# Transfers within DRAM at other places, single-bank PSUM tiles, and an earlier split of operand sums, in a hybrid encoder step

## The chip, the cores and the metric

The kernel runs on one core of one Trainium2 chip. The metric is the device time of one execution in microseconds. The core has a matrix engine (TensorE, PE in the profile), a vector engine (VectorE, DVE), an engine for activations (ScalarE, ACT), a general engine (GpSimd, POOL) and a sequencer that issues transfers (SyncE, SP). Transfers from GpSimd go by a queue that software fills (q0 in the profile), those from SyncE by a hardware queue (q1).

## The reference

One step of a one-layer streaming encoder on 512 prompt frames and 32 frames of a running stream. Half of the mixer's heads are a gated recurrence, half are latent attention; then comes a convolutional FFN.

```python
def token_mixer(x, s0, lat_past, kr_past, ...):
    hq, hf, hi, hg, cq, ckv, kr = jnp.split(x @ w_in, SPLITS, axis=-1)
    f = lb + (1.0 - lb) * jax.nn.sigmoid(hf)
    o_h, s_new = hgrn2_recurrence(heads(hq), heads(1.0 - f), heads(jnp.log(f)), heads(hi), s0, blk)
    o_h = rms_norm(o_h, hgrn_norm_g) * jax.nn.silu(hg)
    ...
    o_a = mla_attention(q_nope, q_rope, k_nope, krs, v, q_pos, k_pos)
    out = jnp.concatenate([o_h, o_a], axis=-1) @ w_out
    return out, s_new, lat_new, kr_new

h = layer_norm(x)
h = layer_norm(ALPHA * h + token_mixer(h))
h = layer_norm(ALPHA * h + conv_ffn(h))
```

`w_in` is 2048 x 4928, `w_out` 2048 x 2048, and the FFN is 5632 wide; everything is float32.

## The kernel before

**Precision and tiling.** The 544 frames lie along the free dimension, as two halves of 272. Each float32 operand is split into a high and a low part (`aH`, `aL` for activations, `wh`, `wl` for weights: a copy to `fp32r` on ScalarE, a subtraction on VectorE), and each product is three matmuls, high by high, high by low and low by high (`mm3`, L146).

**Stages** (by the timeline of the profiled execution): input norm and the query latent until about 80 us; the key and value latent and the rotary key (`ckv_proj`, `kr_proj`, `head_qf(0)`) until 141; four pairs of attention heads, `proj_pair` woven with `attend`, and `head_ig(0)` until about 305; the levels of the first recurrence heads with the sums of inputs (`load_sums` L721 and L722, `sums_of_inputs` with the subtractions of L181) until 371; the recurrence with the divided input projection until about 710; the first column group of the output projection (`out_first`) until 745; the rest of the output projection until about 866; then the FFN (L1313, L1344). In the recurrence, each head's norm takes a power on GpSimd (L995).

**Divided products.** Some projections are computed block by block with sums of weight blocks and sums of activations, so that a 2 x 2 block product takes seven products in place of eight. In the input projection the summed weights are formed in SBUF by accumulating DMAs of GpSimd (L782 in `form`, L795 in `low`). For the output projection, sixteen summed blocks of `w_out` (`wf_dr`) are formed inside DRAM by 32 transfers, a copy or an accumulate of 512 KB each (`forming`, L79 to L97). They come in six phases: eight copies, eight accumulates, then four each of copies, accumulates, copies and accumulates. `form_next` issues the next one. All of them go out on GpSimd: 16 from `tick` in the attention stage, every fourth step (L672 to L687), and 16 from `low` behind the accumulate of product s2: two each time while more than eight are left, then one.

**The block products of the output projection.** Eight steps of `five` and `six` (`step`, L1467 on) compute column groups five and six plainly for the first half of the frames, beside the first norm sums (`Norm.first`, L1121 to L1149). Then `play` runs the list `oitems`, one `Product` (L1794) after the other. Four products "11" come first, one for each group g, and each writes a PSUM tile `X[g]`; `out_sink` (L1825, L1822) adds the result to the residual on VectorE. `ohooks` names what VectorE and ScalarE do after an item: the splits of the summed activations (`split_su`, L1417 and L1418) among them.

**What sets the order.** Inside `manual_schedule` each engine runs what the program writes, in that order. A queue of transfers is in order at its issuing engine. A matmul waits until the earlier readers of its PSUM tile are done, by tile and not by half: X[1] and X[2] are the two halves of one tile of two banks, and X[3] and X[4] of another.

Of the kernel before, what the change touches and what calls it, by code (L numbers as in the profile page):

```python
# [59 lines left out]
def tile_encoder_step(ctx, tc, xp, xs, w_in, w_in4, w_kr, w_q_b, w_kv_b, w_out, w_out4, w_up, w_gate, w_down, w_down2,  # L60
# [24 lines left out]
    def forming(phase):  # L85
        for g in range(1, 5):
            f = {n: wf_dr[g, n] for n in ("s1", "s2", "s3", "22")}
            for out, src, add in ((("s1", "11", False), ("s3", "12", False)), (("s1", "12", True), ("s3", "22", True)),
                                  (("s2", "s1", False),), (("s2", "22", True),), (("22", "s2", False),), (("22", "21", True),))[phase]:
                src = f[src] if src in f and not add else out_block(g, src)  # L90
                yield lambda out=f[out], src=src, add=add: G.dma_start(out, src, **({"accum_op": ALU.add, "max_dma_last_dim": 2048} if add else {}))
# [3 lines left out]
    def form_next(n=0):  # L95
        if len(forms) > n:
            tc.keep_in_program_order(forms.pop(0)())  # L97
# [302 lines left out]
    with tc.tile_pool(name="mp", bufs=1) as mp, tc.tile_pool(name="psa", bufs=4, space=PSUM) as psa:  # L400
# [271 lines left out]
        weave([ckv_proj(), kr_proj()], [cq_norm()], 0.5)  # L672
        weave([head_qf(0)], [ckv_norm(), kr_rope()], 0.5)
        ticks = [0]

        def tick():
            ticks[0] += 1
            if ticks[0] % 4 == 0:
                form_next(16)

        weave([proj_pair(0)], [], 0.0, tick)
        weave([proj_pair(1)], [attend(0)], 2.0, tick)
        weave([proj_pair(2)], [attend(1)], 2.0, tick)
        weave([proj_pair(3)], [attend(2)], 2.0, tick)
        weave([head_ig(0)], [attend(3)], 2.0, tick)
        while len(forms) > 16:
            form_next()  # L687

# [14 lines left out]
    with tc.tile_pool(name="gp", bufs=1) as gp, tc.tile_pool(name="psg", bufs=1, space=PSUM) as psg:  # L703
# [60 lines left out]
        class Divided:  # L764
# [26 lines left out]
            def low(self, wh):  # L791
                wl = wp.tile([P, 1024], R, name="wl", tag="wl")
                V.tensor_tensor(out=wl, in0=self.t(self.key), in1=wh.bitcast(F32), op=ALU.subtract)  # L793
                if self.name == "s2":
                    G.dma_start(self.t("11"), self.src("21"), accum_op=ALU.add)  # L795
                    for _ in range(2 if len(forms) > 8 else 1):
                        form_next()
# [294 lines left out]
    psA = ctx.enter_context(tc.tile_pool(name="psA", bufs=2, space=PSUM))  # L1092
# [383 lines left out]
    early = [psA.tile([P, 1024], F32, name="acc", tag="acc") for _ in range(2)]  # L1476
    with tc.manual_schedule():
# [21 lines left out]
        for j in range(2):  # L1499
# [3 lines left out]
            firsts.append(nrm[j].first(zt[0], zt[1], early[0][:, 512 * j:512 * j + 512]))  # L1503
# [6 lines left out]
        five, six = pair_half(early[1], 0), pair_half(main_tile(), 0)  # L1510
# [286 lines left out]
    with tc.manual_schedule():  # L1797
# [37 lines left out]
        xa, xb = main_tile(), main_tile()  # L1835
        X = {g: (xa, xb)[(g - 1) // 2][:, 512 * ((g - 1) % 2):512 * ((g - 1) % 2) + NI] for g in range(1, 5)}
        BC = [psA.tile([P, 1024], F32, name="acc", tag="acc")[:, 512 * i:512 * i + NI] for i in range(2)]
# [19 lines left out]
        def restore():  # L1857
            for k in range(HK):
# [3 lines left out]
        ohooks = {0: [lambda: split_su("s1", 0), lambda: split_su("s1", 1)], 1: [lambda: split_su("s2", 0)], 2: [lambda: split_su("s2", 1)],  # L1862
                  3: [lambda: split_su("s4", 0)], 4: [lambda: split_su("s4", 1)], 5: [lambda: split_21(range(4))],
                  6: [lambda: split_21(range(4, 8))],
# [8 lines left out]
        oitems[1].prep()  # L1873
# [762 lines left out]
```

## Time and profile before

| | us |
|---|---|
| median of 3 runs | 2353.41 |
| lowest and highest | 2353.05, 2353.92 |
| profiled execution | 2357.51 |
| its span in the profile | 2355.7 |

The page of the profile gives the share of the span in which each engine works, the granted clock of the matrix engine, and the share of time that the 16 DMA engines move something. VectorE works for 73% of the span, ScalarE for 47%, GpSimd for 12%; the DMA engines moved 474.55 MB at a mean of 201 GB/s. In a row of a timeline, the number in square brackets is how long the engine stood idle before, and behind the arrow is what released it. "L1794" is a line of the kernel before.

### The profile page before, as it was taken

What the parts mean: (1) busy time and instruction counts of PE and PEld (TensorE: products, weight loads), DVE (VectorE), ACT (ScalarE), POOL (GpSimd) and SP (SyncE); (2) the same over time, 40 slices, a digit from 0 to 9 for tenths busy, and PEclk for the clock granted to TensorE, in tenths of its full rate; (3) what the DMA queues carried; (4) which work ended last, traced back from release to release, by engine and by line L of the source; (5) the groups of instructions that cost most, each with busy time, mean ns of one, the idle gap of its engine ahead of it and who ended that gap; (6) DMA issues with size and microseconds to landing.
All of it is one profiled execution on the core that took longest, in us unless ns stands there. A gap on an engine that the chain in (4) does not pass through costs nothing.

```text
span 2355.7 us, 44621 instructions
## 1 busy us (share of the span) xinstructions
PE 2304.0 (98%) x18244; PEld 2285.7 (97%) x18244; DVE 1714.7 (73%) x2395; ACT 1095.9 (47%) x1686; POOL 273.9 (12%) x343
## 2 busy tenths in 40 slices
PE   7999999999999999999999999999999999999997
PEld 7999899999999999999999999999999999999996
DVE  7455558777776778987777777777777677777776
ACT  6344434433344536665455554555545433333323
POOL 1011101110111121000010000100001111111102
PEclk9999999999999999999999999999999999999998
DMA  7344475665666655777767667676677999889832
GB/s 245 99 137 128 113 211 166 165 173 165 154 177 229 240 164 201 195 228 192 222 166 227 186 184 222 167 225 187 184 222 185 366 325 306 268 274 301 286 94 78
DMA packets 175772, 474.55 MB, mean 201 GB/s; under 512 B 16080, under 2 KB 80336, under 8 KB 168144
## 3 DMA queue, kind: packets, MB, share of 16 engines
q1 hardware_dynamic: 140112, 316.57, 38.7%
q0 software_dynamic: 35456, 155.14, 28.5%
q8 instruction: 143, 2.34, 0.4%
q14 instruction: 61, 0.50, 0.1%
HBM read 394.36 MB, written 91.34 MB: 206 GB/s over the span
## 4 chain that ended last, share of the span: by engine, by line
PE 90%; DVE 3%; DMA 3%; ACT 2%; issue 1%; POOL 0%; SPq 0%; ACTq 0%; DVEq 0%; POOLq 0%
PE main L1313 21%; PE acc L1313 16%; PE main L1344 10%; PE main L146 10%; PE main L851 10%; PE acc L1344 7%; PE acc L146 3%; PE main L1794 2%; PE s L916 2%; PE acc L1794 2%; PE main L591 1%; PE at L652 1%; DMA cx<-catd 1%; PE at L621 1%; DMA x<-in_xp 1%
## 5 line engine op out<-in xcount | busy, mean ns | idle before, releaser
L1255 DVE TENSOR_TENSOR wl<-raw,wh 128x1024 fp32r<-128x1024 f32 x371 | 456.6, 1231 | 194.4 <-ACT wh L1254 194.1
L1254 ACT ACTIVATE wh<-raw 128x1024 fp32r<-128x1024 f32 x371 | 392.0, 1059 | 410.9 <-PE main L1313 98.4
L1313 PE MATMUL main<-op,wh 128*128 128x272 f32 x1408 | 265.4, 288 | 0.0
L1313 PE MATMUL acc<-ops,wh 128*128 128x272 f32 x1344 | 254.1, 288 | 0.0
L1313 PE MATMUL main<-ops,wh 128*128 128x272 f32 x1344 | 254.1, 288 | 0.0
L1313 PEld LDWEIGHTS main<-op,wh 128*128 128x128 f32 x1408 | 221.1, 188 | 0.0
L1313 PEld LDWEIGHTS acc<-ops,wh 128*128 128x128 f32 x1344 | 211.2, 188 | 0.0
L1313 PEld LDWEIGHTS main<-ops,wh 128*128 128x128 f32 x1344 | 211.1, 188 | 0.0
L1313 PE MATMUL main<-op,wl 128*128 128x272 f32 x704 | 203.1, 289 | 0.3 <-DVE wl L1255 0.3
L1313 PE MATMUL acc<-ops,wl 128*128 128x272 f32 x672 | 194.0, 289 | 0.6 <-DVE wl L1255 0.6
L1313 PE MATMUL main<-ops,wl 128*128 128x272 f32 x672 | 193.9, 289 | 0.0
L1313 PE MATMUL acc<-op,wh 128*128 128x272 f32 x832 | 157.5, 288 | 1.0 <-DVE eg L1619 1.0
L1254 ACT ACTIVATE wh<-rawl 128x1024 fp32r<-128x1024 f32 x93 | 98.8, 1063 | 117.5 <-PE acc L1313 46.1
L146 PE MATMUL main<-aH,wl 128*128 128x272 f32 (+2 forms) x608 | 148.5, 295 | 2.6 <-DVE wl L317 1.8
L146 PE MATMUL main<-aH,wh 128*128 128x272 f32 (+2 forms) x608 | 149.7, 297 | 0.3 <-ACT wh L316 0.2
L146 PE MATMUL main<-aL,wh 128*128 128x272 f32 (+2 forms) x608 | 146.8, 293 | 1.0 <-DVE aL L305 1.0
L1255 DVE TENSOR_TENSOR wl<-rawl,wh 128x1024 fp32r<-128x1024 f32 x93 | 113.8, 1224 | 26.5 <-ACT wh L1254 26.4
L1313 PEld LDWEIGHTS main<-op,wl 128*128 128x128 f32 x704 | 132.4, 188 | 0.5 <-DVE wl L1255 0.5
L1313 PEld LDWEIGHTS acc<-op,wh 128*128 128x128 f32 x832 | 130.6, 188 | 1.2 <-ACT eg L1646 1.2
L793 DVE TENSOR_TENSOR wl<-raw,wh 128x1024 fp32r<-128x1024 f32 x84 | 103.1, 1227 | 35.9 <-ACT wh L788 35.0
L1313 PEld LDWEIGHTS acc<-ops,wl 128*128 128x128 f32 x672 | 126.4, 188 | 0.8 <-DVE wl L1255 0.8
L1313 PEld LDWEIGHTS main<-ops,wl 128*128 128x128 f32 x672 | 126.4, 188 | 0.0
(495 smaller groups left out, 6108.7 us busy)
## 6 DMA issues: line engine op xcount, KB each, us to landing
raw<-in_w_in SPq DMA_DIRECT2D x76, 512.0 KB, 5.1
raw<-in_w_up SPq DMA_DIRECT2D x71, 512.0 KB, 5.3
raw<-in_w_gate SPq DMA_DIRECT2D x71, 512.0 KB, 4.8
raw<-in_w_down SPq DMA_DIRECT2D x67, 512.0 KB, 9.4
opd<-ohl SPq DMA_DIRECT2D x20, 1088.0 KB, 5.5
ops<-opd POOLq DMA_DIRECT2D x20, 1088.0 KB, 12.1
raw<-in_w_up POOLq DMA_DIRECT2D x35, 512.0 KB, 5.3
opd<-ohl SPq DMA_DIRECT2D x20, 816.0 KB, 6.5
```

The source lines that it names most:

```text
L146: PE.matmul(ps, ww[:, wcols[0]:wcols[1]], aa[:, hs[j]], start=first and i == 0, stop=last and i == 2, skip_group_check=True)
L591: PE.matmul(ps[:, j * 512:j * 512 + 256], l[k][:, a:b], r4(w[:, k:k + 1, :])[:, 0, :, 128:256], start=k == 0 and i == 0, stop=k == 1 and i ...
L621: PE.matmul(sc[:, :nk], qn[j][:, q0:q0 + P], kn[j][:, :nk], start=True, stop=False)
L652: PE.matmul(po[:, :P], vt[:, k, j, :], t[:, k * P:(k + 1) * P], start=k == 0, stop=k == b)
L793: V.tensor_tensor(out=wl, in0=self.t(self.key), in1=wh.bitcast(F32), op=ALU.subtract)
L851: PE.matmul(out, ww[:, k * P:(k + 1) * P], aa, start=name in ("11", "s1", "12") and k == 0 and q == 0, stop=k == HK - 1 and q == 2, skip_g ...
L916: PE.matmul(ps[:, j * 64:(j + 1) * 64], Kp[:, a:b], Qv[:, j * bt:(j + 1) * bt, 1, :], start=True, stop=True)
L1254: A.activation(wh, src, AF.Copy)
L1255: V.tensor_tensor(out=wl, in0=src, in1=wh.bitcast(F32), op=ALU.subtract)
L1313: PE.matmul(ps, ww[:, k * P:(k + 1) * P], aa, start=self.first and k == 0 and i == 0, stop=k == n - 1 and i == 2, skip_group_check=True)
L1344: PE.matmul(banks[:, 512 * u:512 * u + NI], ww[:, (u * n + k) * P:(u * n + k + 1) * P], aa, start=self.first and k == 0 and i == 0, stop=k ...
L1794: PE.matmul(self.bank, ww[:, k * P:(k + 1) * P], aa, start=self.first and k == 0 and i == 0, stop=k == HK - 1 and i == 2, skip_group_check ...
```

## The change

Three things are altered. The eight copies of the first phase go out on SyncE's queue instead of GpSimd's, at every fifth step of the latent stage; the attention stage issues none of the 32 transfers; and the other 24 go out in pairs at the twelve s2 points of the recurrence. In the block products, the norm's first sums, `five` and the four tiles `X` get four PSUM tiles of a single bank each (`sb0` to `sb3`, pool `psB`), the two-bank pool `psA` is opened after that stage, and `BC` is now two tiles of the main pool. And the two splits of s1 stand ahead of the last additions of `six`, before `play`, while the later hooks each come one item earlier.

```diff
--- before.py
+++ after.py
@@ -88,7 +88,7 @@
             for out, src, add in ((("s1", "11", False), ("s3", "12", False)), (("s1", "12", True), ("s3", "22", True)),
                                   (("s2", "s1", False),), (("s2", "22", True),), (("22", "s2", False),), (("22", "21", True),))[phase]:
                 src = f[src] if src in f and not add else out_block(g, src)
-                yield lambda out=f[out], src=src, add=add: G.dma_start(out, src, **({"accum_op": ALU.add, "max_dma_last_dim": 2048} if add else {}))
+                yield lambda out=f[out], src=src, add=add: (G.dma_start(out, src, accum_op=ALU.add, max_dma_last_dim=2048) if add else (dma if phase == 0 else G.dma_start)(out, src))
 
     forms = [f for phase in range(6) for f in forming(phase)]
 
@@ -669,22 +669,22 @@
             G.tensor_tensor(out=o[:, :, :NI], in0=o[:, :, :NI], in1=o[:, :, NI:], op=ALU.subtract)
             dma(d3_dr[pr], o[:, :, :NI])
 
-        weave([ckv_proj(), kr_proj()], [cq_norm()], 0.5)
-        weave([head_qf(0)], [ckv_norm(), kr_rope()], 0.5)
         ticks = [0]
 
         def tick():
             ticks[0] += 1
-            if ticks[0] % 4 == 0:
-                form_next(16)
-
-        weave([proj_pair(0)], [], 0.0, tick)
-        weave([proj_pair(1)], [attend(0)], 2.0, tick)
-        weave([proj_pair(2)], [attend(1)], 2.0, tick)
-        weave([proj_pair(3)], [attend(2)], 2.0, tick)
-        weave([head_ig(0)], [attend(3)], 2.0, tick)
-        while len(forms) > 16:
+            if ticks[0] % 5 == 0 and len(forms) > 24:
+                form_next()
+
+        weave([ckv_proj(), kr_proj()], [cq_norm()], 0.5, tick)
+        weave([head_qf(0)], [ckv_norm(), kr_rope()], 0.5, tick)
+        while len(forms) > 24:
             form_next()
+        run(proj_pair(0))
+        weave([proj_pair(1)], [attend(0)], 2.0)
+        weave([proj_pair(2)], [attend(1)], 2.0)
+        weave([proj_pair(3)], [attend(2)], 2.0)
+        weave([head_ig(0)], [attend(3)], 2.0)
 
     def out_piece(kk, g):
         return piece(w_out[kk, max(g - 4, 0)], 4, 256)
@@ -793,7 +793,7 @@
                 V.tensor_tensor(out=wl, in0=self.t(self.key), in1=wh.bitcast(F32), op=ALU.subtract)
                 if self.name == "s2":
                     G.dma_start(self.t("11"), self.src("21"), accum_op=ALU.add)
-                    for _ in range(2 if len(forms) > 8 else 1):
+                    for _ in range(2):
                         form_next()
                 elif self.name not in ("11", "s1"):
                     slots.append(self.raw.pop(self.key)[0])
@@ -1089,7 +1089,6 @@
     ph1.close()
 
 
-    psA = ctx.enter_context(tc.tile_pool(name="psA", bufs=2, space=PSUM))
     seq = [0]
 
     def acc_tile():
@@ -1473,7 +1472,11 @@
                     kk == 0 and k == 0, kk == 3 and k == 3)
 
     ko = [CAT_ORDER[4 * kk] // 4 for kk in range(4)]
-    early = [psA.tile([P, 1024], F32, name="acc", tag="acc") for _ in range(2)]
+    psb_stack, psb = stack(tc.tile_pool(name="psB", bufs=1, space=PSUM))
+
+    def small_tile(n):
+        return psb.tile([P, 512], F32, name=f"sb{n}", tag=f"sb{n}")
+
     with tc.manual_schedule():
         order56 = [(kk, g) for g in (5, 6) for kk in ko]
         raws56, ws56 = [], []
@@ -1500,14 +1503,14 @@
             for t in range(2):
                 z = zt[t][:, H_[j]]
                 V.scalar_tensor_tensor(out=z, in0=z, scalar=ALPHA, in1=wo_tiles[t][:, PS_[j]], op0=ALU.mult, op1=ALU.add)
-            firsts.append(nrm[j].first(zt[0], zt[1], early[0][:, 512 * j:512 * j + 512]))
+            firsts.append(nrm[j].first(zt[0], zt[1], small_tile(j)))
             next(firsts[j])
 
         def next_firsts():
             for f in firsts:
                 next(f, None)
 
-        five, six = pair_half(early[1], 0), pair_half(main_tile(), 0)
+        five, six = [small_tile(2 + t)[:, :NI] for t in range(2)], pair_half(main_tile(), 0)
         step(five, ws56[0], 0, 0)
         split_next()
         next_firsts()
@@ -1832,9 +1835,8 @@
             return Product(out_weights(g, name), name, None, bank, name in ("11", "s1", "12"),
                            lambda: out_sink(g, name, bank))
 
-        xa, xb = main_tile(), main_tile()
-        X = {g: (xa, xb)[(g - 1) // 2][:, 512 * ((g - 1) % 2):512 * ((g - 1) % 2) + NI] for g in range(1, 5)}
-        BC = [psA.tile([P, 1024], F32, name="acc", tag="acc")[:, 512 * i:512 * i + NI] for i in range(2)]
+        X = {g: small_tile(g - 1)[:, :NI] for g in range(1, 5)}
+        BC = [main_tile()[:, :NI] for _ in range(2)]
         oitems = [out_item(g, "11", X[g]) for g in range(1, 5)]
         for g in range(1, 5):
             oitems += [out_item(g, name, {"12": BC[0], "s1": BC[1], "s4": BC[1]}.get(name, X[g]))
@@ -1859,9 +1861,8 @@
                 load_21(k, cat_dr[4 + k // 2][:, k % 2, NI:])
 
         NO = len(oitems)
-        ohooks = {0: [lambda: split_su("s1", 0), lambda: split_su("s1", 1)], 1: [lambda: split_su("s2", 0)], 2: [lambda: split_su("s2", 1)],
-                  3: [lambda: split_su("s4", 0)], 4: [lambda: split_su("s4", 1)], 5: [lambda: split_21(range(4))],
-                  6: [lambda: split_21(range(4, 8))],
+        ohooks = {0: [lambda: split_su("s2", 0)], 1: [lambda: split_su("s2", 1)], 2: [lambda: split_su("s4", 0)],
+                  3: [lambda: split_su("s4", 1)], 4: [lambda: split_21(range(4))], 5: [lambda: split_21(range(4, 8))],
                   NO - 2: [lambda: split_seventh(0)],
                   NO - 1: [lambda: split_seventh(1), lambda: [shifted(14 + t, 0) for t in range(2)]]}
         pump()
@@ -1871,6 +1872,8 @@
         oitems[0].prep()
         step(six, ws56[7], 0, 3)
         oitems[1].prep()
+        for i in range(2):
+            split_su("s1", i)
         for t in range(2):
             V.tensor_tensor(out=zt[12 + t][:, H_[0]], in0=zt[12 + t][:, H_[0]], in1=six[t], op=ALU.add)
             fill(0.8, lambda t=t: nrm[0].add(zt[12 + t], G))
@@ -1883,6 +1886,8 @@
             drain(3.0)
 
     ou_stack.close()
+    psb_stack.close()
+    psA = ctx.enter_context(tc.tile_pool(name="psA", bufs=2, space=PSUM))
     st_stack, st = stack(pool("st", "right"))
 
     with tc.manual_schedule():
```

On GpSimd, from the third attention pair to the setup of the recurrence, before (L91 is a transfer within DRAM into a summed block `wf`; L669 is the subtraction at the end of a pair; L560, L462 and L567 belong to the rotary embedding):

```order
L560 COPY ql_964<-t 128x32
L91 DMA wf1s_101<-in_w_out 256x512
L91 DMA wf2s_103<-in_w_out 256x512
L669 TENSOR_TENSOR o<-o 128x2x272
L91 DMA wf2s_105<-in_w_out 256x512
L91 DMA wf3s_107<-in_w_out 256x512
L91 DMA wf3s_109<-in_w_out 256x512
L669 TENSOR_TENSOR o<-o 128x2x272
L91 DMA wf4s_111<-in_w_out 256x512
L91 DMA wf4s_113<-in_w_out 256x512
L708 MEMSET attnT_3489 128x544
L708 MEMSET attnT_3490 128x544
```

The same place of the changed kernel:

```order
L560 COPY ql_964<-t 128x32
L462 TENSOR_TENSOR t<-t,cos 128x544
L567 COPY ql_964<-t 64x32 x2
L560 COPY ql_964<-t 128x32
L669 TENSOR_TENSOR o<-o 128x2x272 x2
L708 MEMSET attnT_3481 128x544
L708 MEMSET attnT_3482 128x544
L711 MEMSET kT 128x128
```

All transfers L91 of this place are gone; they were accumulates, and they stand in the recurrence now.

On GpSimd, the last points s2 of the recurrence, before (L782 and L795 are the accumulates into weights in SBUF, L995 the power in a head's norm, and the last row loads the residual for the output projection):

```order
L782 DMA raw<-in_w_in 128x1024
L795 DMA raw<-in_w_in 128x1024
L91 DMA wf_110<-in_w_out 256x512
L995 TENSOR_TENSOR r_7624<-r_7623,nhalf 128x5
L782 DMA raw<-in_w_in 128x1024
L795 DMA raw<-in_w_in 128x1024
L91 DMA wf_114<-in_w_out 256x512
L995 TENSOR_TENSOR r_8226<-r_8225,nhalf 128x5
L1495 DMA za<-h0d_69 128x544
```

and in the changed kernel:

```order
L91 DMA wf_102<-in_w_out 256x512
L91 DMA wf_106<-in_w_out 256x512
L995 TENSOR_TENSOR r_7623<-r_7622,nhalf 128x5
L782 DMA raw<-in_w_in 128x1024
L795 DMA raw<-in_w_in 128x1024
L91 DMA wf_110<-in_w_out 256x512
L91 DMA wf_114<-in_w_out 256x512
L995 TENSOR_TENSOR r_8226<-r_8225,nhalf 128x5
L1498 DMA za<-h0d_69 128x544
```

Each point has two accumulates within DRAM where it had one, and the last summed block is the second of its pair. The number of points with an L995 behind them stays.

On the matrix engine, the heads of the first two block products, with the semaphores that they wait for (Activation is ScalarE, DVE is VectorE; the first row of each group opens a product), before:

```order
L1794 MATMUL main<-aH,wh 128x272 [waits Activation_49]
L1794 MATMUL main<-aL,wh 128x272
L1794 MATMUL main<-aH,wl 128x272 [waits DVE_49]
...
L1794 MATMUL main<-aH,wh 128x272 [waits DVE_49,Activation_49]
L1794 MATMUL main<-aL,wh 128x272
L1794 MATMUL main<-aH,wl 128x272
```

and in the changed kernel, where L1797 is the former L1794:

```order
L1797 MATMUL sb_8711<-aH,wh 128x272 [waits Activation_49]
L1797 MATMUL sb_8711<-aL,wh 128x272
L1797 MATMUL sb_8711<-aH,wl 128x272 [waits DVE_49]
...
L1797 MATMUL sb_8712<-aH,wh 128x272 [waits Activation_49]
L1797 MATMUL sb_8712<-aL,wh 128x272
L1797 MATMUL sb_8712<-aH,wl 128x272 [waits DVE_49]
```

The second product no longer waits for VectorE at its first matmul; it waits for it two matmuls later, for its low weights, as the first one does.

## The prediction

> **What bounds the kernel now.** I read the page first, then the waits of TensorE (PE), then the granted clock by window, then the timeline around each long wait.
>
> ```profile
> span 2355.7 us, 44621 instructions
> PE 2304.0 (98%) x18244; PEld 2285.7 (97%) x18244; DVE 1714.7 (73%) x2395; ACT 1095.9 (47%) x1686; POOL 273.9 (12%) x343
> ```
>
> PE is busy for 98% of the span, so only two things can shorten the time without removing matmuls: an idle gap of PE, or a stretch in which its clock is lowered. The waits of PE, as total, count and longest in us, hold five rows that the change can reach:
>
> ```profile
> PE main L1794 <- DVE za L1825: 4.4, 2, 3.8
> PE at L638 <- DVE o L653: 2.4, 1, 2.4
> PE s L916 <- DVE Kp L922: 3.0, 1, 3.0
> PE acc L1126 <- ACT n_cb L1140: 0.5, 1, 0.5
> PE acc L1121 <- DVE nt_c L1136: 0.3, 1, 0.3
> ```
>
> Windows say what follows them. The columns are the length, busy times and counts of the engines, the granted clock (PEclk), the share of the DMA engines, and GB/s:
>
> ```profile
> 240.00:250.00 10.00, 8.35 (x42) 7.45 (x43) 7.80 (x19) 5.68 (x13) 3.02 (x5) 0.83 0.63 131
> ...
> 310.00:320.00 10.00, 7.00 (x50) 6.78 (x49) 6.21 (x16) 2.15 (x5) 2.09 (x4) 0.90 1.03 300
> 320.00:330.00 10.00, 10.00 (x54) 10.00 (x53) 5.31 (x14) 1.49 (x2) 0.00 (x0) 0.59 0.92 275
> 770.00:780.00 10.00, 6.17 (x48) 5.98 (x47) 7.12 (x9) 7.82 (x9) 2.42 (x2) 0.94 1.03 411
> 780.00:790.00 10.00, 9.38 (x54) 9.19 (x54) 5.96 (x7) 3.59 (x4) 0.00 (x0) 0.72 0.73 284
> ```
>
> After each of the three waits of 2.4 us or more the clock falls below 1.00 for a while. A stretch at clock c loses (1 − c) of its length: 0.17 × 10 = 1.7 us behind the wait in attention, 0.10 × 10 + 0.41 × 10 = 5.1 us behind the one at the levels, 0.06 × 10 + 0.28 × 10 = 3.4 us behind the one in the block products, 3.4 on average. So a removed wait is worth itself plus this. By the Trainium skill, page "TensorE: Matmul & The Clock Gate", section "What's actually happening", half rate follows an idle window of about 3.4 us and full rate returns after a busy window of about 3.4 us; the trace differs, since 2.41 us already sufficed here and the clock stayed low longer at the levels. By the page a spell would cost an estimated 1.7 us instead of these measured losses, and the forecast gain would be 10.0 instead of 13.4.
>
> **Block products: single-bank tiles and earlier splits (gain 7.4 + 0.8).**
>
> ```profile
> 772.58 0.28 PE L1794 MATMUL main<-aH,wh 128*128 128x272 f32 x1
> ...
> 775.14 3.06 DVE L1418 TENSOR_TENSOR us<-us 128x1088 fp32r<-128x1088 f32 x2
> ...
> 779.02 0.43 DVE L1825 SCALAR_TENSOR_TENSOR za<-za,main 128x272 f32<-128x272 f32 x1
> 779.36 1.22 DVE L1255 TENSOR_TENSOR wl<-raw,wh 128x1024 fp32r<-128x1024 f32 x1
> ...
> 779.59 0.56 PE L1794 MATMUL main<-aH,wh 128*128 128x272 f32 x1 [3.83 <-DVE za L1825]
> ...
> 780.50 1.28 DVE L1418 TENSOR_TENSOR us<-us 128x1088 fp32r<-128x1088 f32 x1
> ```
>
> The first block product starts at 772.58. The second writes the other half of the same two-bank tile, so it waits until DVE has read the first half (L1825, 779.02), and DVE is held up by two operand splits of s1 (3.06 us for the pair). PE stands for 3.83 us. The fourth product does the same with the second tile:
>
> ```profile
> 789.19 0.36 PE L1794 MATMUL main<-aH,wh 128*128 128x272 f32 x1 [0.62 <-DVE za L1825]
> ...
> 738.62 6.12 PE main L146 x48
> ```
>
> The undisturbed price of a product of 24 matmuls is half of the row of 48 on the chain of waits: 3.06 us. The three products from 772.58 to 789.19 should take 9.18 and took 16.61, so 7.4 us are lost, in idle time and slow clock together. In the new order the waits on VectorE at the heads of products two and four are gone; both write tiles of their own. What is late next? DVE has per product one sink (0.43), one weight split (1.22) and one operand split (1.28), 2.93 us against 3.06 on PE, so it just keeps up, and the weight splits needed for the second product are behind fewer operations than before, since the s1 splits now stand ahead of play. These two splits there run beside the last two steps of `six`, 48 matmuls or 6.1 us, against 2 × 1.5 us. If that cover were gone they would cost 3.06. I take the whole 7.4; the bounds are 0, if DVE stays the bound, and 7.4. The two waits of the norm's first sums (0.5 and 0.3, rows above) come from one shared tile too and go: 0.8, between 0 and 0.8.
>
> **Attention without transfers within DRAM (gain 4.1).**
>
> ```profile
> 227.93 0.94 POOL L91 DMA_DIRECT2D wf1s<-in_w_out  x1
> ...
> 232.89 0.59 SPq L458 DMA_DIRECT2D t<-t  x1
> ...
> 238.67 0.72 DVE L463 TENSOR_TENSOR t<-t,sin 128x544 f32<-128x544 f32 x1 [3.59 <-DMA t<-t]
> ...
> t<-t SPq DMA_DIRECT2D x20, 68.0 KB, 2.1
> ```
>
> The swap of rows for the rotary embedding is issued at 232.89 and DVE gets it at 238.67, 5.8 us later; the median of its kind, from issue to landing, is 2.1 (the last line, from the list of DMA issues). In front of it, at 227.93, GpSimd issued an accumulate within DRAM. DVE stands 3.59 us for the swap, and the attention copy of L653 queued behind it makes PE stand 2.4 (its row among the waits above). At the median the swap would land 3.7 us earlier, more than the stall. Removed: 2.4 + 1.7 of slow clock = 4.1. The bounds are 0 (the swap is late because of the weight loads beside it) and 4.1; I take 4.1, since the accumulate is the only transfer of that kind in that stretch.
>
> **Sums of inputs (gain 7.5).**
>
> ```profile
> 303.06 0.87 POOL L91 DMA_DIRECT2D wf4s<-in_w_out  x1
> ...
> 306.92 1.53 SPq L721 DMA_DIRECT2D s<-h0d  x3
> ...
> 313.10 0.44 DVE L181 TENSOR_TENSOR s_f<-s,s 128x272 f32<-128x272 f32 x1 [4.76 <-DMA s<-h0d]
> ...
> s<-h0d SPq DMA_DIRECT2D x32, 136.0 KB, 3.8
> ```
>
> The same again: an accumulate at 303.06, three loads from 306.92 on, of which the first sum needs two, and DVE standing 4.76 us until 313.10. Behind L181 and its followers on DVE waits L922, and on it PE, 3.0 us (its row among the waits above). The second load is issued at about 307.4; at the median of its kind, 3.8 us (last line), it lands at 311.2, 1.9 us earlier, and at the 2.1 us of the smaller swap at 309.5, 3.6 us earlier. The gain is 1.9 to 3.0 of idle time and 5.1 of slow clock: 7.0 to 8.1, and 0 if the loads delay each other. I take the middle, 7.5.
>
> **What the moved transfers cost where they go.** The eight copies of the first phase are issued on SyncE's queue in the latent stage:
>
> ```profile
> 80.00:141.00 61.00, 60.80 (x490) 60.61 (x489) 27.53 (x45) 17.42 (x25) 5.21 (x4) 1.00 0.36 108
> ```
>
> PE is busy for 60.80 of these 61 us, at full clock and a DMA share of 0.36 (columns as in the windows above). Queued behind the copies on SP are the next weight loads; they are hidden by the weights that are already split, so the cost is 0. Without that cover one copy would delay a load as the swap above was delayed: 3.7 us, with a slow clock 7. In the recurrence, each s2 point now issues two transfers where the last eight points had one. An accumulating pair holds GpSimd:
>
> ```profile
> 439.75 1.26 POOL L91 DMA_DIRECT2D wf1s<-in_w_out  x1
> ...
> 449.41 0.90 POOL L91 DMA_DIRECT2D wf2s<-in_w_out  x1 [8.39 <-issue]
> ...
> 456.39 1.19 POOL L995 TENSOR_TENSOR r<-r,nhalf 128x5 f32<-128x5 f32 x1 [6.08 <-DVE r L994]
> ```
>
> From 439.75 to 450.3 GpSimd is held, 10.6 us, and the next operation that matters there, the power in the head's norm at 456.39 (L995), comes 16.6 us after the first issue. It stays 6 us clear: cost 0; the other end is the last rival's 30. The price is at the last point, where the second accumulate now falls ten microseconds after 687.53, into a stretch that is already full:
>
> ```profile
> 687.53 1.29 POOL L91 DMA_DIRECT2D wf<-in_w_out  x1
> ...
> 690.00:698.00 8.00, 8.00 (x69) 8.00 (x69) 5.94 (x13) 2.48 (x4) 0.00 (x0) 1.00 1.01 200
> 698.00:710.00 12.00, 12.00 (x101) 12.00 (x100) 9.44 (x23) 4.25 (x8) 0.00 (x0) 1.00 1.05 400
> ...
> 708.59 1.07 ACT L134 ACTIVATE wh<-raw 128x1024 fp32r<-128x1024 f32 x1 [3.45 <-DMA raw<-in_w_out]
> ...
> 716.18 0.52 PE L146 MATMUL main<-aH,wl 128*128 128x272 f32 x2 [0.88 <-DVE wl L135]
> ...
> q0 software_dynamic: 35456, 155.14, 28.5%
> ```
>
> The rows are from the timeline, from two windows (columns as above), and from the page's list of queues (packets, MB, share of the span). DMA share is 1.01 at 200 GB/s while the accumulate runs and 1.05 at 400 GB/s after it. ScalarE stands 3.45 us for a weight load at 708.59, and PE has a gap of 0.88 us behind a weight split at 716.18. One more accumulate of 512 KB takes at least 0.524 MB divided by the software queue's own rate, 155.14 MB in 28.5% of 2355.7 us = 231 GB/s: 2.3 us. At most it halves the rate for 8 us, as the first window shows: 4.0 us, and a third more for the read of the target, 5.3. I take 3.0, nearer to the queue's rate, because that rate already contains many accumulates. The gap becomes 3.9 us, and gaps of 2.4 and more were followed by a slow clock, so 3.4 more: −6.4 (bounds 0, hidden, and −10). By the Trainium skill, page "DMA: Bandwidth & Descriptors", section "Issuing engines are not separate DMA queues", transfers run on the same sixteen engines whichever engine issues them. That speaks against this change, which moves load and removes none; the trace agrees as far as the two rates above show. By it alone the sum would be the 1.8 of the second rival below.
>
> **The sum.** 7.4 + 0.8 + 4.1 + 7.5 − 6.4 = 13.4 us. The profiled execution took 2357.5, of which its span is 2355.7, so 2344.1 for it; the median of the runs is 2353.4, 4.1 lower, and the same gain gives 2340.0.
>
> **Rivals.**
> - The extra accumulate at the end of the recurrence is hidden: the last term is 0, and the time 2333.6. For it: PE itself has a gap of only 0.88 us there. Against it: the share of 1.05. 22%.
> - Attention and sums do not improve, because the loads that are late there wait behind 512 KB weight loads and one another on engines that all transfers share, and the accumulates were only a part of it; at the end of the recurrence the cost stays. The gain is 8.2 − 6.4 = 1.8, and the time 2351.6. For it: the share is 1.03 in 310 to 320, at 300 GB/s. Against it: both late transfers follow an accumulate by 4 to 5 us. (This is where the rule of the DMA page leads.) 10%.
> - DVE stays the bound of the block products (2.93 against 3.06 is little room), 7.4 is not had: 2347.4. 12%.
> - Slower: the pairs of accumulates hold GpSimd for 20 us instead of 10.6, and L995 comes late. It decides from a hold of 16.6 us, and at the first call from 13.4:
>
> ```profile
> 384.60 0.84 POOL L91 DMA_DIRECT2D wf1s<-wf1s  x1
> ...
> 397.95 1.18 POOL L995 TENSOR_TENSOR r<-r,nhalf 128x5 f32<-128x5 f32 x1 [12.01 <-DVE r L994]
> ```
>
> Four of the accumulating calls have an L995 behind them. At 20 us the first loses 6.6 and three lose 3.4 each, with a slow clock of 3.4 behind all four: 16.8 + 13.6 = 30.4, and the time is 2370.4. The measured 10.6 speaks against it. 6%.
>
> **How the numbers follow.** The forecast has 50%. The range 2332 to 2351 takes in the forecast with both ends of its terms, the hidden accumulate and the DVE-bound block products, together 84%. A measurement tells 0.2%, or 4.7 us, from no change: faster is below 2348.7, slower above 2358.1. Forecast, first and most of the third rival are faster: 0.80. The second and the rest of the third are the same: 0.13. Slower is the fourth and one hundredth for what I overlooked: 0.07.
>
> **What would show it.** Right would be: no wait of PE on L1825's successor between the first block products and clock 1.00 in 770 to 790; no wait of L638 on L653 and of L916 on L922; and a wait at the first pieces of the output projection longer than 0.9 us. Wrong would be a wait of PE for DVE at another place in the block products, a swap or sum that lands late without an accumulate in front, or L995 with PE waiting behind it.

## The result, and the profile after

The changed kernel takes 2339.99 us (median of 4, 2339.09 to 2340.97) against 2353.66 of the kernel before on the same chip (median of 4, 2353.05 to 2357.07): a ratio of 0.9939, with a 95% interval from 0.9922 to 0.9956. That is 13.7 us. The profiled execution took 2339.57, its span is 2337.8.

The page, and the rows of the waits of the matrix engine that answer to those shown before (total, count, longest, in us):

```profile
span 2337.8 us, 44618 instructions
...
PE 2295.4 (98%) x18244; PEld 2279.1 (97%) x18244; DVE 1713.6 (73%) x2395; ACT 1095.4 (47%) x1686; POOL 271.1 (12%) x335
```

```profile
PE main L1797 <- DVE za L1828: 1.4, 1, 1.4
PE sw L952 <- DVE Kp L922: 1.1, 1, 1.1
...
PE main L146 <- ACT wh L134: 1.0, 1, 1.0
PE main L146 <- DVE wl L135: 0.9, 1, 0.9
```

The rows of L638 on L653 (2.4), of L916 on L922 (3.0) and of the two first sums of the norm (0.5 and 0.3) are gone. The row of the block products has shrunk from 4.4 to 1.4 and is another wait than before: a product that comes five places later. Two rows at the first pieces of the output projection are new or longer: 1.0 on ScalarE, and 1.1 instead of 0.5 on L922.

The windows of before, again with length, busy times, clock, DMA share and GB/s, and one more at the end of the recurrence:

```profile
240.00:250.00 10.00, 10.00 (x67) 8.62 (x66) 6.99 (x22) 6.03 (x14) 0.21 (x1) 1.00 0.41 127
310.00:320.00 10.00, 10.00 (x85) 10.00 (x85) 7.85 (x20) 1.92 (x3) 0.00 (x0) 1.00 0.86 257
320.00:330.00 10.00, 10.00 (x83) 9.79 (x84) 7.95 (x19) 4.46 (x9) 0.00 (x0) 1.00 0.76 239
...
700.00:710.00 10.00, 7.05 (x41) 6.45 (x40) 9.07 (x16) 8.81 (x17) 0.00 (x0) 0.83 0.49 146
770.00:780.00 10.00, 10.00 (x80) 9.80 (x79) 7.74 (x11) 6.64 (x11) 0.00 (x0) 1.00 0.90 346
780.00:790.00 10.00, 8.65 (x70) 8.66 (x70) 8.31 (x15) 5.01 (x8) 0.00 (x0) 1.00 0.60 203
```

The clock is 1.00 in the five windows that had 0.59 to 0.94. It is 0.83 in a new place, 700 to 710. The two transfers that had been late are on time now, by the timeline:

```profile
231.56 0.59 SPq L458 DMA_DIRECT2D t<-t  x1
...
234.40 0.73 DVE L463 TENSOR_TENSOR t<-t,sin 128x544 f32<-128x544 f32 x1 [0.26 <-DMA t<-t]
```

```profile
301.08 1.38 SPq L721 DMA_DIRECT2D s<-h0d  x3
...
304.77 0.44 DVE L181 TENSOR_TENSOR s_f<-s,s 128x272 f32<-128x272 f32 x1 [1.36 <-DMA s<-h0d]
```

The swap is used 2.8 us after its issue (5.8 before), and the first sum starts 3.7 us after the loads are issued (6.2 before).

**Where the time went.** The matrix engine runs the same number of matmuls in both kernels, 18244, so the n-th matmul of one profile can be set beside the n-th of the other. The table gives the difference of their start times (after minus before) at the ends of the stages. A second profile of each kernel (runs e4 and e11 below) gives the second pair. (The output projection's first four products are named "11"; s1 and s4 are later products of a group, and the s4 product is the seventh in order.)

| up to matmul | stage that ends there | first pair | second pair |
|---|---|---|---|
| 110 | start | +0.3 | −0.5 |
| 1700 | attention | −5.2 | −3.6 |
| 2270 | sums and first levels | −13.1 | −9.3 |
| 5680 | recurrence, `out_first` | −10.1 | −5.7 |
| 5730 | first sums of the norm | −10.8 | −6.4 |
| 5950 | first block products | −18.4 | −12.6 |
| 6030 | s4 product of the first group | −16.8 | −11.3 |
| 18000 | FFN | −18.2 | −10.8 |

### The profile page after: what moved, and what is told of

It reads as the page before. It is cut to its first block, busy times and chain, and to the rows that moved or that the text cites. A ratio compares the mean times of both kernels' runs of the same rounds, so it can differ in the third digit from the quotient of the medians.

```text
span 2337.8 us, 44618 instructions
## 1 busy us (share of the span) xinstructions
PE 2295.4 (98%) x18244; PEld 2279.1 (97%) x18244; DVE 1713.6 (73%) x2395; ACT 1095.4 (47%) x1686; POOL 271.1 (12%) x335
## 4 chain that ended last, share of the span: by engine, by line
PE 92%; DVE 2%; ACT 2%; DMA 2%; issue 1%; SPq 0%; POOL 0%; ACTq 0%; DVEq 0%; POOLq 0%
PE main L1312 22%; PE acc L1312 17%; PE main L146 11%; PE main L1343 11%; PE main L851 10%; PE acc L1343 7%; PE acc L146 3%; PE s L916 2%; PE main L1797 1%; PE sb L1797 1%; PE main L591 1%; PE at L652 1%; PE at L621 1%; DMA cx<-catd 1%; DMA xr<-wf1s 1%
```

## The experiments

Ratios are against the kernel before on the same chip, five rounds each; in brackets the 95% interval.

**The three parts alone.** First the transfers:

```diff
-                form_next(16)
...
+            if ticks[0] % 5 == 0 and len(forms) > 24:
+                form_next()
...
-                    for _ in range(2 if len(forms) > 8 else 1):
+                    for _ in range(2):
```

with the copies of the first phase on SyncE, as in the change.

> The transfers within DRAM at their new places, PSUM tiles and split order as before. My theory: the accumulates beside attention are what makes the rotary swap (L458) and the loads of the sums (L721) late. From the matmuls of the two profiles, aligned one by one, attention gives 5.5 us, the sums 7.9, and the end of the recurrence takes back 3.1: a span 10.3 us shorter than the profiled 2355.7, no wait of L638 on L653 and none of L916 on L922, and the wait of the second block product (3.8 us) still there. Rival: the loads delay one another whatever the accumulates do; then the waits on L653 and L922 stay and the gain is under 3 us.

Measured: 2347.08 against 2354.30, 0.9970 (0.9960 to 0.9981), and a span of 2344.9, 10.8 below the profiled 2355.7. By the medians that is 7.2 us. The waits on L653 and L922 are gone, and so is 1.2 us of a wait on a softmax step (L604); the wait of the second block product is still 3.8. The rival falls.

Then the tiles:

```diff
-        five, six = pair_half(early[1], 0), pair_half(main_tile(), 0)
+        five, six = [small_tile(2 + t)[:, :NI] for t in range(2)], pair_half(main_tile(), 0)
...
-        X = {g: (xa, xb)[(g - 1) // 2][:, 512 * ((g - 1) % 2):512 * ((g - 1) % 2) + NI] for g in range(1, 5)}
-        BC = [psA.tile([P, 1024], F32, name="acc", tag="acc")[:, 512 * i:512 * i + NI] for i in range(2)]
+        X = {g: small_tile(g - 1)[:, :NI] for g in range(1, 5)}
+        BC = [main_tile()[:, :NI] for _ in range(2)]
```

> The single-bank PSUM tiles alone; transfers and split order as before. My theory: the shared two-bank tile is the whole cause of the stall, since the low weights of the first three block products are ready before the s1 splits: no wait of PE on L1825 at the second and fourth product, clock 1.00 in 770 to 790, and 7 to 8.4 us shorter (0.8 of it from the norm's first sums). Rival: VectorE is the bound, because two splits of 1.5 us each still stand ahead of the first sink and the weight split behind it; then PE waits for low weights instead of the sink and the gain is under 4 us.

Measured: 2347.28 against 2354.30, 0.9969 (0.9956 to 0.9981). By the medians that is 7.0 us. Both waits of PE at the second and fourth product are gone, and the clock stays up. The only row of a block product that is left, of 0.5, belongs to the s4 product. From its waits, its timeline and its windows:

```profile
PE main L1797 <- DVE za L1828: 0.5, 1, 0.5
```

```profile
789.13 0.49 PE L1797 MATMUL main<-us,wh 128*128 128x272 f32 x2 [0.46 <-DVE za L1828]
```

```profile
770.00:780.00 10.00, 10.00 (x82) 10.00 (x81) 9.15 (x12) 7.61 (x9) 2.41 (x2) 1.00 1.02 408
```

So the shared tile alone was the cause, and VectorE was not the bound of the first four products. The two s1 splits still stand ahead of the first sink here, and cost nothing.

Then the order of the splits:

```diff
+        for i in range(2):
+            split_su("s1", i)
...
-        ohooks = {0: [lambda: split_su("s1", 0), lambda: split_su("s1", 1)], 1: [lambda: split_su("s2", 0)], 2: [lambda: split_su("s2", 1)],
...
+        ohooks = {0: [lambda: split_su("s2", 0)], 1: [lambda: split_su("s2", 1)], 2: [lambda: split_su("s4", 0)],
```

> The earlier s1 splits alone; transfers and tiles as before. My theory: the tile dependence stays, but VectorE reaches the first sink 3.1 us earlier, so that the wait of 3.8 us falls to about 0.8 and, being that short, brings no slow clock; the second wait (0.6) stays: about 6 us shorter. Rival: the order has no effect of its own, because the sink waits for other work on VectorE as well (weight split 1.7, norm 1.0): the wait stays above 2 us and the gain is under 3.

Measured: 2353.10 against 2354.30, 0.9993 (0.9984 to 1.0002): nothing that these runs can tell from no change. My expectation was wrong. The row of its waits:

```profile
PE main L1794 <- DVE za L1825: 3.2, 2, 2.6
```

The longest wait went from 3.8 to 2.6 and not to 0.8. VectorE, ahead of the first sink:

```profile
772.50 1.85 DVE L1418 TENSOR_TENSOR us<-us 128x1088 fp32r<-128x1088 f32 x1
774.28 0.98 DVE L1162 TENSOR_TENSOR n_s<-n_s,n_e 128x272 f32<-128x272 f32 x2
775.17 0.43 DVE L1825 SCALAR_TENSOR_TENSOR za<-za,main 128x272 f32<-128x272 f32 x1
```

The two s1 splits (3.06 us) moved away, but the hook that came one item earlier put a split of s2 (1.85 us) in their place. The difference of 1.2 us is what the wait lost. The sink still stood behind work of VectorE, as the rival said.

**The changed kernel without the early splits**, the other two parts kept:

```diff
-        for i in range(2):
-            split_su("s1", i)
...
-        ohooks = {0: [lambda: split_su("s2", 0)], 1: [lambda: split_su("s2", 1)], 2: [lambda: split_su("s4", 0)],
...
+        ohooks = {0: [lambda: split_su("s1", 0), lambda: split_su("s1", 1)], 1: [lambda: split_su("s2", 0)], 2: [lambda: split_su("s2", 1)],
```

> The changed kernel without the earlier s1 splits: transfers moved, single-bank tiles, split order as before. My theory: with the tiles apart the order has nothing left to gain at the second product; what it does is to bring the splits of split_21 ahead of the sink of s1, so that without it the new wait at the s4 product falls from 1.0 to 1.5 us to about 0.5 (as with the tiles alone) and the time is within 1.5 us of the changed kernel, on the faster side. Rival: the order still hides the s1 splits, and a wait of over 1.5 us comes back between 765 and 780.

Measured: 2340.38 against 2354.58, 0.9937 (0.9924 to 0.9951), the changed kernel's own ratio within the intervals. The wait at the s4 product is 0.4 us here:

```profile
PE main L1797 <- DVE za L1828: 0.4, 1, 0.4
```

Of the three edits, two carry the change: by the medians the transfers alone gain 7.2 us and the tiles alone 7.0, and the kernel with both gains 14.2. The third gains nothing beside the tiles. With the hooks that it brings forward the wait at the s4 product is 1.4 and 1.0 us in the two profiles of the changed kernel, where it is 0.4 here.

**The kernel before, once more.**

> The kernel before, unchanged, for a second profile of it. The profiled execution took 2357.5 and the median of its runs is 2353.5. Theory: the difference sits in one of the waits with a slow clock behind it (most of all the one at the sums, 3.0 plus 5.1, or in attention, 2.4 plus 1.7), which differ from one execution to the next; then this profile has a shorter wait there and a span near 2352. Rival: the difference is spread evenly, or lies at the input and the end; then all three waits are the same within 0.3 us.

Measured: 2353.79, ratio 0.9999 (0.9991 to 1.0008), a span of 2351.2, 4.5 below that of the first profile. The three waits are as long as in the first profile, within 0.3 us:

```profile
PE main L1794 <- DVE za L1825: 4.5, 2, 3.8
PE s L916 <- DVE Kp L922: 3.3, 1, 3.3
...
PE at L638 <- DVE o L653: 2.2, 1, 2.2
```

```profile
240.00:250.00 10.00, 8.05 (x45) 6.50 (x45) 7.81 (x19) 5.38 (x12) 3.32 (x5) 1.00 0.59 121
...
310.00:320.00 10.00, 6.71 (x43) 6.49 (x43) 6.24 (x16) 2.15 (x5) 2.09 (x4) 0.80 1.03 288
320.00:330.00 10.00, 10.00 (x75) 10.00 (x74) 6.91 (x18) 1.49 (x2) 0.00 (x0) 0.86 0.89 269
...
770.00:780.00 10.00, 6.16 (x38) 5.97 (x37) 8.90 (x10) 6.17 (x8) 2.41 (x2) 0.84 1.03 411
780.00:790.00 10.00, 9.38 (x74) 9.19 (x74) 6.99 (x8) 5.70 (x7) 0.00 (x0) 0.99 0.66 232
```

What differs is the clock behind them. Attention lost 1.7 us to it in the first profile and loses 0 here; the levels lost 5.1 and lose 2.0 + 1.4 = 3.4; the block products lost 3.4 and lose 1.6 + 0.1 = 1.7. Together 10.2 against 5.1. The theory's place was right, its reason wrong: between these two executions the waits hardly differ, and what the clock makes of them does. A wait can differ too, though. In e2, whose attention issues the same work as before, the wait on L653 was longer:

```profile
PE at L638 <- DVE o L653: 3.7, 1, 3.7
```

**The changed kernel, once more.**

> The changed kernel, unchanged, for times on the same chip and a second profile. Theory: its waits at 690 to 710 (3.0 us in sum) and at the s4 product (1.4) are the same within 0.3 us, and only the number of slow spells of the clock differs, in steps of 1.7 us: span 2336 to 2340. Rival: the waits themselves differ from one execution to the next.

Measured: 2340.53 against 2355.56, 0.9938 (0.9927 to 0.9950), span 2338.7. The waits at the end of the recurrence are 3.6 us in sum (3.0 in the first profile), the one at the s4 product 1.0 (1.4), and one slow spell of 1.7 us follows the former in both. So the waits vary by some tenths too, more than I expected.

**Accumulates or copies.** The kernel before, with only the accumulates out of attention:

```diff
-                form_next(16)
+                form_next(24)
...
-        while len(forms) > 16:
+        while len(forms) > 24:
...
-                    for _ in range(2 if len(forms) > 8 else 1):
+                    for _ in range(2):
```

> The kernel before with one edit: attention issues only the eight copies, on GpSimd as before; the eight accumulates go in pairs to the s2 points. My theory: it is the accumulates and not transfers within DRAM as such that delay the swap and the sums' loads, so that the waits on L653 and L922 go as with all transfers moved: 12 to 13 us earlier when the sums are done, and 9 to 10 us in all. Rival: copies do the same harm; then a wait of over 1 us is seen in an earlier pair, or the gain by the end of the sums is under 8.

Measured: 2348.39 against 2355.21, 0.9967 (0.9955 to 0.9980). By the end of the sums it is 10.9 us ahead of the first profile of before, where 12 to 13 were expected; it is 12.8 with all transfers moved (e1), both by the count of matmuls; against the second profile of before (e4) the two are 8.3 and 10.2. The whole gain by the medians is 6.8 us, less than the 9 to 10 expected. The wait on L653 is gone, and of two others a part stays:

```profile
PE s L916 <- DVE Kp L922: 1.2, 1, 1.2
...
PE at L638 <- ACT p L604: 1.0, 1, 1.0
```

So the accumulates did most of the harm. The wait on the softmax step L604 (1.2 before) stands among the copies and is gone where these go too (e1). One of 0.5 shows in the second profile of the changed kernel, which has no copies there, so that the copies cause it is not shown. Why 1.2 us stay at the levels, with no transfer within DRAM near, isn't settled either. By what path an accumulate delays the small transfers beside it is not shown by any run.

**Who issues the copies.** In `forming` the copies go back to GpSimd, at the same steps:

```diff
-                yield lambda out=f[out], src=src, add=add: (G.dma_start(out, src, accum_op=ALU.add, max_dma_last_dim=2048) if add else (dma if phase == 0 else G.dma_start)(out, src))
+                yield lambda out=f[out], src=src, add=add: (G.dma_start(out, src, accum_op=ALU.add, max_dma_last_dim=2048) if add else G.dma_start(out, src))
```

> The changed kernel with the eight copies of the first phase issued by GpSimd, at the same steps of the latent stage. My theory: the engine that issues them does not matter there, since neither SyncE nor GpSimd is what the matrix engine waits for before attention: within 1 us of the changed kernel, PE busy for over 60 of the 61 us from 80 to 141. Rival: on GpSimd they hold the rotary multiplication (L462) or the power of the latent norms, so that a wait of over 0.5 us appears between 80 and 200.

Measured: 2340.81 against 2355.56, 0.9933 (0.9921 to 0.9945), no different from the changed kernel (0.9938). PE is busy for 60.80 of the 61 us from 80 to 141, as it was before and as it is in the changed kernel. The queue doesn't matter there.

**The end of the recurrence.** In the profile of the changed kernel the last pair stands so on GpSimd, and ScalarE waits for the first weights of the output projection:

```profile
674.49 1.29 POOL L91 DMA_DIRECT2D wf<-in_w_out  x1
685.57 0.89 POOL L91 DMA_DIRECT2D wf<-in_w_out  x1 [9.79 <-issue]
...
697.33 1.06 ACT L134 ACTIVATE wh<-raw 128x1024 fp32r<-128x1024 f32 x1 [5.24 <-DMA raw<-in_w_out]
...
701.87 0.49 PE L146 MATMUL main<-aH,wh 128*128 128x272 f32 x2 [0.96 <-ACT wh L134]
```

ScalarE stands 5.24 us (3.45 before). To take the accumulates away from there, the four copies of a phase go out at one point, and the list ends two points earlier:

```diff
-                    for _ in range(2):
+                    for _ in range(4 if len(forms) in (16, 8) else 2):
```

> The changed kernel, with the four copies of a phase at one s2 point in place of two, so that the last two points issue nothing. My theory: the second accumulate at the last point costs 3.1 us at the first pieces of the output projection (1.6 of waits, 1.7 of slow clock), and the first one some of the 1.4 of waits that were there before: 3 to 4.5 us faster than the changed kernel, its three waits at 690 to 710 under 1 us in sum. Rival: the weight loads and the 18 loads of cx delay one another and the accumulate is hidden; then it is within 1 us of the changed kernel. Second rival: four copies at once hold GpSimd or the DMA engines, and a wait appears at 500 to 630.

Measured: 2334.85 against 2355.21, 0.9912 (0.9897 to 0.9927). Against 0.9939 for the changed kernel that is about 6 us, more than the 3 to 4.5 expected. In the two profiles the gain at this place is 5.2 us by the count of matmuls, of which the waits (3.0) and the slow clock (1.7) make 4.7. All three waits are gone, the 1.4 us of before with them, and so is the slow spell. The same window of the changed kernel and of this one:

```profile
680.00:698.00 18.00, 18.00 (x151) 18.00 (x150) 12.30 (x29) 5.68 (x10) 0.89 (x1) 1.00 1.05 322
```

```profile
680.00:698.00 18.00, 18.00 (x151) 18.00 (x150) 13.52 (x32) 9.93 (x17) 0.00 (x0) 1.00 0.82 303
698.00:710.00 12.00, 12.00 (x102) 11.79 (x101) 11.60 (x18) 9.37 (x15) 0.00 (x0) 1.00 0.49 159
```

The DMA share falls from 1.05 to 0.82 in 680 to 698, and no wait appears at the points that issue four copies. Both rivals fall.

**The new wait in the block products.** VectorE in the changed kernel:

```profile
779.39 1.49 DVE L1426 TENSOR_TENSOR aL<-aL,aH 128x272 fp32r<-128x272 f32 x4
780.80 0.43 DVE L1828 SCALAR_TENSOR_TENSOR za<-za,main 128x272 f32<-128x272 f32 x1
...
781.37 0.49 PE L1797 MATMUL main<-us,wh 128*128 128x272 f32 x2 [1.35 <-DVE za L1828]
```

The s4 product shares its tile with s1 and waits for the sink of s1, and four small splits stand ahead of that sink. Moved one item later:

```diff
-                  3: [lambda: split_su("s4", 1)], 4: [lambda: split_21(range(4))], 5: [lambda: split_21(range(4, 8))],
+                  3: [lambda: split_su("s4", 1)], 5: [lambda: split_21(range(4))], 6: [lambda: split_21(range(4, 8))],
```

> The changed kernel with the two split_21 hooks one item later, as they stood before. My theory: the new wait of 1.4 us at the s4 product of the first group (on the sink of s1, which shares its tile) comes because VectorE does the four splits of split_21 (1.5 us) ahead of that sink, so that it goes and the kernel is 1 to 1.6 us faster. Rival: VectorE is late because the weights of the s1 product (a load that landed at 774.5) came late; then the wait stays within 0.5 us.

Measured: 2339.88 against 2355.21, 0.9930 (0.9918 to 0.9943). The wait is gone from the profile, and at its place in the table of matmuls nothing is lost any more, where the two pairs lost 1.6 and 1.3 us; in the median nothing of it can be told from the spread of the runs. Both of the last edits together:

> The two edits before together: if they are independent, the sum of their gains against the changed kernel, 4 to 6 us by my theories and about 2335; if the wait at the end of the recurrence was cover for the block products' loads, less than the sum.

Measured: 2333.25 against 2355.21, 0.9906 (0.9892 to 0.9919). It has the lowest ratio of all, about 8 us below the changed kernel's by 0.9906 against 0.9939, where 4 to 6 were expected; between 150 and 900 us its longest wait of the matrix engine is 0.8. Against e6 alone it is 1.6 us lower, within what the intervals leave open.

**How long GpSimd may be held.** In the changed kernel the first pair ends just in time:

```profile
371.45 1.31 POOL L91 DMA_DIRECT2D wf1s<-in_w_out  x1
382.18 0.89 POOL L91 DMA_DIRECT2D wf1s<-in_w_out  x1 [9.42 <-issue]
384.88 1.19 POOL L995 TENSOR_TENSOR r<-r,nhalf 128x5 f32<-128x5 f32 x1 [1.81 <-DVE r L994]
```

The hold is 382.18 + 0.89 − 371.45 = 11.6 us, and 1.8 us later L995 starts, on time. With three accumulates at this point and one at the next:

```diff
-                    for _ in range(2):
+                    for _ in range({24: 3, 21: 1}.get(len(forms), 2)):
```

> The changed kernel with three accumulates at the first s2 point and one at the second, the rest as it is. This makes the hold of GpSimd longer where the room is least: in the changed kernel the second accumulate was out at 383.1 and the power L995 started at 384.9. My theory (the slower rival of the prediction): the third is issued about 10.7 us after the second, so that L995 comes about 9 us late, VectorE stands at L999, and PE waits: 4 to 7 us of waits between 385 and 400, with one to three slow spells of 1.7 us behind them, 6 to 12 us slower. Rival: GpSimd does not hold, or L995 is not on the way: no wait of over 1 us there.

Measured: 2344.25 against 2355.56, 0.9952 (0.9940 to 0.9965), 3.7 us above the changed kernel on the same chip. Its GpSimd and VectorE:

```profile
384.14 0.89 POOL L91 DMA_DIRECT2D wf1s<-in_w_out  x1 [9.84 <-issue]
390.37 0.90 POOL L91 DMA_DIRECT2D wf2s<-in_w_out  x1 [5.33 <-issue]
390.96 1.54 POOL L995 TENSOR_TENSOR r<-r,nhalf 128x5 f32<-128x5 f32 x1
```

```profile
392.53 0.82 DVE L999 TENSOR_TENSOR sqg<-sw,r 128x640 f32<-128x640 f32 x1 [4.74 <-POOL r L995]
```

```profile
PE main L851 <- DVE hproj L839: 1.8, 1, 1.8
```

The chain is as told: the third accumulate is issued late, L995 stands behind it, VectorE stands 4.74 us for it, and the matrix engine 1.8, with one slow spell. In the profiles this kernel loses 3.6 us against the changed one at this place, by the count of matmuls. The size was wrong: I had 4 to 7 us of waits and 6 to 12 in all. The third accumulate came 6.2 us after the second and not 10.7, and the matrix engine had work for most of the rest.

## Why the prediction came true, point by point

The time was 2340.0 as forecast, and the two largest gains came by the mechanisms named. The sizes did not all come true; that the sum fits to a tenth is partly luck. In us, from the table of matmuls:

| term | forecast | first pair | second pair |
|---|---|---|---|
| attention | −4.1 | −5.5 | −3.1 |
| sums of inputs | −7.5 | −7.9 | −5.7 |
| end of the recurrence | +6.4 | +3.0 | +3.6 |
| first sums of the norm | −0.8 | −0.7 | −0.7 |
| first block products | −7.4 | −7.6 | −6.2 |
| s4 product | none | +1.6 | +1.3 |

- **Block products.** The cause was right, and e2 shows it: with tiles of their own the second and fourth product don't wait. I had put the earlier splits beside the tiles as a part of the gain. They are none (e3, e12): I overlooked that the hooks brought forward put a split of s2 where those of s1 had been. That VectorE "just keeps up" was right for the first products, and too tight for the seventh, where hooks that were brought forward stand ahead of a sink that it needs. One of the signs that I had named for being wrong, a wait for VectorE at another place in the block products, did appear. This is the third rival in small: 1.0 to 1.4 us instead of 7.4.
- **Attention and sums.** Right, and shown by e1 and e5: the second rival, that weight loads and not the accumulates were the cause, falls. In attention I left out a wait on L604 of 1.2 us, which goes in the first pair and shrinks from 1.4 to 0.5 in the second.
- **End of the recurrence.** The step was right in its place and its sign, and mis-sized. I took 3.0 us of waits and 3.4 of slow clock. Measured were 1.6 us more of waits (3.0 for 1.4; I had counted only 0.9 of these 1.4), and 1.7 of slow clock. e6 shows that the cause is the accumulates at the last points: without them all of it goes. The first rival, that it is hidden, falls. The outer bound of −10 does not come out of its terms, 5.3 and 3.4; nothing else rests on it.
- **The slow clock.** The step that failed is "a removed wait is worth itself plus this", with a fixed price of the clock and a condition, a gap of 2.4 us or more. The profiled execution before had lost 10.2 us to it; another profile of the same kernel lost 5.1 with the same waits (e4). The forecast took the gain of 10.2 and applied it to the median, which is some way between. The terms for gains were 19.8 in sum, where the two pairs show 21.7 and 15.7, 18.7 on the mean; the terms for losses were 6.4, where they show 4.6 and 4.9. So 1.1 us too much of gain stand against 1.6 too much of loss. The condition failed as well: a wait of 2.6 us in e3 was followed by no slow clock, and three waits of 0.9 to 1.1 us in the changed kernel were. At 1.7 us a wait, which is the mean in e4 and the cost at the new place, the forecast's sum comes to 10.0 and not 13.4, so that the fit of the sum says little for the price of 3.4.
- **The slower rival.** Its mechanism exists (e10) and its place was right, at the first point. It did not happen, since a pair holds GpSimd for 11.6 us and L995 is due after 13.4. Its price was set too high: L995 came 4.6 us after its operand was there (391.0 against 386.3) and that cost 1.8 us of wait and one spell of 1.7, where the rival would have had 4.6 + 3.4.
- **The copies in the latent stage.** Cost 0, as forecast: PE is busy for 60.80 of the 61 us there, before and after. e9 shows that the queue is of no account.

## What to carry to other kernels

When the matrix engine waits for a reader of "its" PSUM tile, look whether the reader reads the same half: with tiles of a bank each, and no other edit, both waits of 4.4 us in sum went (e2). A transfer off the path is cheap or dear by what is beside it: the same accumulates cost waits beside small loads that are used at once, nothing in the middle of the recurrence, and again waits where the DMA engines are already full (a share of 1.05), so that a better place than either of the two was the one that ends earlier (e6, 0.9912). And before a sum is made from one profiled execution, take a second profile of the same kernel: here the waits came out within 0.3 us, and what the slow clock cost behind them was half.

## What the runs showed of the hardware

- The losses to the clock in the middle of the kernel come in steps. They were 1.7, 5.1 and 3.4 us in the first profile of before, 0, 3.4 and 1.7 in the second, 1.7 at the end of the recurrence in the changed kernel (0.17 of 10 us) and 1.7 in e10 between 385 and 400 (0.11 of 15 us). A wait of 2.4 us was once followed by one step, one of 2.2 by none, one of 3.0 by three and one of 3.3 by two; in e3 one of 2.4 and one of 2.6 had none behind them. The Trainium skill, page "TensorE: Matmul & The Clock Gate", section "What's actually happening", has half rate after an idle window of about 3.4 us and full rate after a busy one; half rate through one such window would be an estimated loss of 1.7, which agrees with the size of the step. That an idle window is needed does not agree: three waits of 1.0, 1.1 and 0.9 us, spread over 4 us, were enough in the changed kernel.
- The second of two accumulates within DRAM stood 8.3 to 10.2 us on GpSimd before it was issued, in all eight pairs of the changed kernel; the third in e10 stood 5.3. Two copies followed each other after 0.5 us (592.8 and 593.3 in the changed kernel). What the accumulate waits for isn't shown by these runs.
